# Moving the output gate's weight splits and the sums of the keys' squares to later steps of a mixer's recurrence

## The chip, the cores and the metric

The kernel runs on one core of a Trainium2 chip. Its engines are TensorE (matmul; PE in the profile, its weight loads PEld), VectorE (DVE), ScalarE (ACT), GpSimd (POOL) and SyncE (SP), whose queue issues the DMAs. The metric is the device time of one execution in microseconds; less is better.

## The reference, cut to what matters

Two layers over 128 context tokens and 256 latent tokens (384 in all, 1024 wide), each of them a feed-forward half-step, a token mixer and a second feed-forward half-step. The change is in the mixer, which computes three things from one input projection and joins them in one output projection:

```
z = h @ w_in ; zq, zi, zff, zfb, zg, zglu, cq, ck, cv = split(z)
o_a  = rms_norm(recurrence_fw + recurrence_bw) * silu(zg)        # gated linear recurrence
o_b  = silu(layer_norm(depthwise_conv(glu_a * sigmoid(glu_b))))  # convolution over 31 positions
o_c  = attention(rope(rms_norm(cq)), rope(rms_norm(ck)), cv)     # 8 query heads, 2 key heads
y    = concat(o_a, o_b, o_c) @ w_out
```

`zg` is the output gate. The RMS norm of the keys needs, for each token and key head, the sum of the 64 squares.

## The kernel before, in words

All activations lie on the chip. Each fp32 weight is split into a rounded part and a rest, and a product is three matmuls (high by high, high by low, low by high). Such a split (`prep(n, eng)`, or `wo_prep(k)` for the output weights) is a cast of 128x1024 on ScalarE (L893 in `hi`, L600) and a subtraction on VectorE (L899 in `lo`, L601). Its source is a raw buffer of 1 MB, which SyncE's queue fills. There are four raw buffers under one name (`raw`), which weights, the convolution's blocks (`cw`) and its shifted data (`U[ct]`, written to DRAM at L997 and read back at L1002) share; a buffer is handed on when its last reader is done. Split weights lie in four buffers (`wgu`).

The order of work on TensorE, VectorE, ScalarE and GpSimd is the order in which the program is written; SyncE's queue is ordered by the framework. An instruction waits in its engine's queue for what it needs, and all behind it wait too.

The 384 tokens are three blocks of 128. The recurrence is computed for two pairs of heads (`dec[0]`, `dec[1]`). For each pair, `level(8)`, `level(16)`, `level(32)` and `level(64)` rescale queries and keys with copies on ScalarE (L1123, L1124) and products on VectorE (L1127 to L1130). Then a loop of seven steps `i` does, for pair `i // 3` and token block `i % 3`:

- `scores(i)`: small matmuls (L1200) into one of two PSUM pairs, and four masked copies on VectorE (`copy_predicated`, L1209) into two tiles of scores, `a1` (three of the copies) and `a2` (one);
- `outputs(i - 1)`: matmuls (L1234) of those tiles, first `a2`, then `a1`, with the values, and of the states; after the third block a copy of the result `oS` on ScalarE (L1238);
- besides, by the number of the step: the last levels of the second pair (steps 0 and 1), the convolutions `conv(0)` and `conv(1)` (L1009, steps 2 and 4), the scaling and rotation of the keys (`norm_rope`, L953 to L961, steps 2 to 4), the turn of the second pair's keys `kN` (L1141, L1147, step 3), the states (L1155, step 4), `gh`'s load (step 3), the output weights' loads `wo_load(4)` (step 2, L1410) and `wo_load(6)`, `(0)`, `(2)` (step 5), the splits `wo_prep(4)` and `wo_prep(5)` (step 4), and in step 5 the product for the gate, `zg` (L664), which reads the split weights W[14] and W[15]. Two more `zg` follow in the attention.

Before the change `prep(14)` and `prep(15)`, the splits of the gate's weights, stand in step 0. The sums of squares (`head_ssq`: a square on ScalarE at L936, a reduction on VectorE at L937, and on GpSimd a scaling at L940 and a power at L943), one for each token block, stand ahead of the loop; `norm_rope` reads their results. In what follows a "mixer" is the first or the second layer's (about 330 to 500 us and 1080 to 1250 us of the span).

Of the kernel before, what the change touches and what calls it, by code (L numbers as in the profile page):

```python
# [18 lines left out]
P = 128  # L19
DM = 1024  # L20
KT = 8
NT = 3
# [22 lines left out]
class Net:  # L45
# [815 lines left out]
    def mixer(self, l, eps, nxt):  # L861
# [12 lines left out]
        mp = scope(es, "mix")  # L874
# [29 lines left out]
        def prep(n, eng, pool=None):  # L904
            lo(n, hi(n, pool))
# [11 lines left out]
        kn = self.t(mp, [P, NT, P], "kn")  # L917
# [14 lines left out]
        def head_ssq(x, nh, t1):  # L932

            f = 64 if nh == 8 else 1
            ss = self.t(mp, [P, 16], "ss", bufs=8)
            nc.scalar.activation(t1, x, AF.Square)  # L936
            nc.vector.reduce_sum(  # L937
                ss[:, 0:nh], t1.rearrange("p (h d) -> p h d", d=64), axis=AX.X
            )
            nc.gpsimd.tensor_scalar(  # L940
                ss[:, 0:nh], ss[:, 0:nh], f / 64, f * 1e-6, ALU.mult, ALU.add
            )
            nc.gpsimd.tensor_tensor(  # L943
                ss[:, 8 : 8 + nh], ss[:, 0:nh], self.eps[:, 2:3].to_broadcast([P, nh]), ALU.pow
            )
            return ss
# [191 lines left out]
        def state_turn(p):  # L1138
            pt = self.wbank()
            for i, (d, tok) in enumerate(((0, 0), (0, 1), (1, 0), (1, 2))):  # L1140
                nc.tensor.transpose(  # L1141
                    pt[:, i * P : (i + 1) * P],
                    dec[p].Kc[d][:, tok * P : (tok + 1) * P],
                    self.ident,
                )
            kN = self.t(hp, [P, 4, P], "kN")
            nc.scalar.copy(kN.rearrange("p a b -> p (a b)"), pt)  # L1147
            return kN

        def states(p, kN):  # L1150
            pt = self.wbank()
            for i, tok in enumerate((0, 1, 0, 2)):
                for hh in range(2):
                    rs = slice(64 * hh, 64 * hh + 64)
                    nc.tensor.matmul(  # L1155
                        pt[rs, i * 64 : i * 64 + 64],
                        kN[:, i, rs],
                        vN[:, tok, 128 * p + 64 * hh : 128 * p + 64 * hh + 64],
                        start=True,
                        stop=True,  # L1160
                    )
            S1 = self.t(hp, [P, 4, 64], "S1", bufs=2)
            for i, d in ((0, 0), (2, 1)):
                nc.scalar.copy(S1[:, i, :], pt[:, i * 64 : i * 64 + 64])
                nc.sync.dma_start(
                    self.o["new_state_hgrn"][0, l, d, 2 * p : 2 * p + 2].rearrange(
                        "h d e -> (h d) e"
                    ),
                    S1[:, i, :],
                )  # L1170
            for i, d in ((1, 0), (3, 1)):
                nc.vector.scalar_tensor_tensor(
                    S1[:, i, :], S0[:, d, p, :], dec[p].et[d][:, d + 1 : d + 2],
                    pt[:, i * 64 : i * 64 + 64], ALU.mult, ALU.add,
                )
            return S1
# [3 lines left out]
        def scores(i):  # L1180

            p, tok = divmod(i, NT)
            Qd, Kd, lev = dec[p].D, dec[p].K, dec[p].lev
            tsl = slice(tok * P, (tok + 1) * P)
            a1, a2 = A1[i % 2], A2[i % 2]
            prs = [(Qd[0], Kd[0], a1), (Qd[1], Kd[1], a2)] + [(q_, k_, a1) for q_, k_ in lev]
            if i < 2:
                sbs[i] = self.pair(1 + i)  # L1190
            sb = sbs[i % 2]
            for kd_, m, x in ((0, 32, 0), (1, 32, 0), (2, 32, 0), (3, 32, 0), (4, 32, 32), (5, 64, 64)):
                n = min(kd_, 3)
                if i < 2 and n < 3:
                    m = P
                for hh in range(2):
                    rs = slice(64 * hh, 64 * hh + 64)
                    for c in range(0, P, m):
                        r = c ^ x
                        nc.tensor.matmul(  # L1200
                            sb[c : c + m, hh, n * P + r : n * P + r + m],
                            prs[kd_][1][rs, tok * P + c : tok * P + c + m],
                            prs[kd_][0][rs, tok * P + r : tok * P + r + m],
                            start=True,
                            stop=True,
                            tile_position=(64 * hh, c),
                        )
            for n in range(4):
                nc.vector.copy_predicated(  # L1209
                    prs[n][2],  # L1210
                    self.smask[:, n, :].unsqueeze(1).to_broadcast([P, 2, P]),
                    sb[:, :, n * P : (n + 1) * P],
                )
# [141 lines left out]
        k_ss = []  # L1355
# [35 lines left out]
        glu(1)  # L1391
        S1s = [states(0, kN)]
        dec[1].level(16)
        for tok in range(NT):
            k_ss.append(head_ssq(kn[:, tok, :], 2, self.t(mp, [P, P], "t1k", bufs=2)))
        nc.sync.dma_start(self.o["new_cache_v"][0, l].rearrange("s h d -> s (h d)"), kv[:, 0, :])

        wop, wraw = {}, {}
# [2 lines left out]
        def wo_load(kb):  # L1401
            raw = wraw[kb] = self.t(self.rawp, [P, 2, DM], "raw")
            if kb < 4:
                nc.sync.dma_start(
                    raw, wo[l, kb * P : (kb + 2) * P, :].rearrange("(k p) n -> p k n", p=P)
                )
            else:
                for g in range(2):
                    r0 = 512 + g * 256 + (kb - 4) * 64
                    nc.sync.dma_start(  # L1410
                        raw[64 * g : 64 * g + 64],
                        wo[l, r0 : r0 + 128, :].rearrange("(j p) n -> p j n", p=64),
                    )

        def wo_prep(k, pool, tag, size=2 * DM, lo=nc.vector):
            w = self.t(pool, [P, size], tag, F32R)[:, 0 : 2 * DM]
            w = w.rearrange("p (a n) -> p a n", a=2)
            wop[k] = self.split_to(w, wraw[k // 2 * 2][:, k % 2, :], lo)
# [3 lines left out]
        def keys_turn():  # L1422
            pt = self.wbank()
            for i, src in enumerate((kn[:, 0, :], ck[:, 0, :], kn[:, 1, :], kn[:, 2, :])):
                nc.tensor.transpose(pt[:, i * P : (i + 1) * P], src, self.ident)
            nc.scalar.copy(kT.rearrange("p a b -> p (a b)"), pt)
# [84 lines left out]
        def zg(n):  # L1511

            tok = (1, 0, 2)[n]
            ps = self.wbank()[:, 0:256]
            self.entry_mm((ps,), [[W[14], W[15]]], tok, (0,), range(KT))
            nc.scalar.copy(zs[:, tok, :], ps)
# [3 lines left out]
        def att(n):  # L1520
            units.append(Att(n))
            units[n].scores()

        for i in range(2 * NT + 1):
            if i < 2 * NT:
                scores(i)
            if i == NT + 1:
                S1s.append(states(1, kN))
            if i == NT:
                kN = state_turn(1)  # L1530
            if i == 2 * NT:
                keys_turn()
            if i == 0:
                prep(14, nc.vector)
                prep(15, nc.vector)
            if i == 2:
                wo_load(4)
            if i in CONV_AT:
                conv(CONV_AT[i])
            if i == 5:  # L1540
                wo_load(6)
                wo_load(0)
                wo_load(2)
            if i == 4:
                wo_prep(4, self.wgu, "wgu")
                wo_prep(5, self.wgu, "wgu")
            if i > 0:
                outputs(i - 1)
            if i in HFILL:
                zg(HFILL.index(i))  # L1550
            if i == NT + 1:
                o_turn(0)
            if i == 2 * NT:
                att(0)
                units[0].exp()
            if i == NT:
                es1.close()
                ap_ = scope(es, "at")
                gh = self.t(ap_, [P, 1, 256], "gh")
                nc.sync.dma_start(  # L1560
                    gh[:, 0, :], a["hgrn_norm_g"][l : l + 1, :].to_broadcast([P, 256])
                )
            if i < 2:
                dec[1].level(32 << i)
            elif i < 2 + NT:
                tok = i - 2
                norm_rope(
                    kn[:, tok, :], k_ss[tok], tok, 2, 1, self.t(mp, [P, P], "t1k", bufs=2)
                )
# [233 lines left out]
```

## Time and profile before

| | |
|---|---|
| median of 3 runs | 1535.4 us (1534.51, 1535.40, 1538.37) |
| the profiled execution's own time | 1536.49 us |
| its span | 1534.7 us |
| its mean granted TensorE clock | 0.993 |
| TensorE busy | 1508.5 us, 98% of the span |
| VectorE, ScalarE, GpSimd busy | 69%, 42%, 4% |

The profile is one execution. Times in its rows are counted from the start of the span, in us. An instruction's row may show in brackets how long its engine stood idle before it and what ended that wait; "issue" there means that nothing in the profile shows what it waited for. A granted clock of 1 is full speed.

### The profile page before, as it was taken

Reading aid. Unit: us, or ns where it says so; the run is one execution under the profiler, and the core shown is the slowest. Engines: PE = TensorE matmul, PEld = TensorE weight load, DVE = VectorE, ACT = ScalarE, POOL = GpSimd, SP = SyncE. Lnnn points to the kernel's source line nnn. Section 1 sums busy time; section 2 is a strip of 40 time slices with the busy share of each in tenths; the row PEclk is TensorE's granted clock in tenths of the full one; section 3 lists DMA queues with packets and bytes.
Section 4 is the critical chain, followed back from the end, with each engine's and each line's share of the span. In section 5 each row is a group of like instructions: output and inputs, shape, how many; then the busy total and the mean of one; then the engine's idle time right before and its main releaser. Section 6 shows DMA issues by size and latency. Waiting matters only on the chain.

```text
span 1534.7 us, 23659 instructions
## 1 busy us (share of the span) xinstructions
PE 1508.5 (98%) x9605; PEld 1345.4 (88%) x9605; DVE 1058.5 (69%) x1525; ACT 649.3 (42%) x1112; POOL 59.3 (4%) x96
## 2 busy tenths in 40 slices
PE   8999999999999999999999999999999999999997
PEld 7989999989677899999989999998986789999996
DVE  4788778679677777777676676675795786554334
ACT  3434333366475533333353333333763764332331
POOL 0000000030101000000000000000210100000001
PEclk9999999999999999999999999999999999999999
DMA  9886766423524456666535465633336146342411
GB/s 379 287 293 223 244 234 228 171 66 136 115 93 165 165 216 238 224 227 209 206 110 220 165 247 181 240 145 122 118 94 169 48 167 249 126 179 110 165 55 41
DMA packets 65732, 271.22 MB, mean 177 GB/s; under 512 B 9224, under 2 KB 15832, under 8 KB 51032
## 3 DMA queue, kind: packets, MB, share of 16 engines
q1 hardware_dynamic: 65624, 269.72, 50.0%
q8 instruction: 75, 1.23, 0.3%
q14 instruction: 33, 0.27, 0.1%
HBM read 266.67 MB, written 3.03 MB: 176 GB/s over the span
## 4 chain that ended last, share of the span: by engine, by line
PE 93%; ACT 2%; DVE 2%; DMA 2%; issue 1%; SPq 0%; POOL 0%; DVEq 0%; POOLq 0%; ACTq 0%
PE w L610 46%; PE d L623 26%; PE d L683 7%; PE d L610 4%; PE w L1009 2%; PE w L664 1%; DMA raw<-w_mod_first 1%; PE w L208 1%; PE d L1200 1%; PE w L427 1%; PE d L1234 1%; ACT Pr L1468 1%; DVE G L196 1%; PE d L1450 1%; PE d L1498 1%
## 5 line engine op out<-in xcount | busy, mean ns | idle before, releaser
L610 PE MATMUL w<-xh,wgu 128*128 128x384 f32 x2720 | 711.9, 337 | 1.0 <-DVE hf L781 1.0
L610 PEld LDWEIGHTS w<-xh,wgu 128*128 128x128 f32 x2720 | 494.3, 188 | 10.5 <-issue 4.9
L610 PE MATMUL w<-xl,wgu 128*128 128x384 f32 x1360 | 455.9, 335 | 0.0
L623 PE MATMUL d<-wo,hh 128*128 128x512 f32 x1056 | 284.3, 391 | 0.0
L196 DVE SCALAR_TENSOR_TENSOR G<-t,cc,G 128x1024 f32<-128x1024 f32 x224 | 272.9, 1280 | 0.0
L610 PEld LDWEIGHTS w<-xl,wgu 128*128 128x128 f32 x1360 | 256.5, 189 | 2.2
L623 PEld LDWEIGHTS d<-wo,hh 128*128 128x128 f32 x1056 | 196.9, 188 | 36.5
L601 DVE TENSOR_TENSOR wgu<-raw,wgu 128x1024 fp32r<-128x1024 f32 x166 | 196.0, 1222 | 35.5 <-ACT wgu L600 35.1
L783 ACT CAST hh<-hf 128x384 fp32r<-128x384 f32 x82 | 42.2, 515 | 345.6 <-DVE hf L781 345.6
L781 DVE TENSOR_TENSOR hf<-w,sg 128x384 f32<-128x384 f32 x79 | 44.0, 557 | 185.2 <-PE w L610 185.2
L600 ACT CAST wgu<-raw 128x1024 fp32r<-128x1024 f32 x166 | 166.2, 1050 | 1.6 <-DMA raw<-ffn_w_in 1.6
L623 PE MATMUL d<-wo,hl 128*128 128x512 f32 x528 | 163.2, 390 | 0.0
L779 ACT ACTIVATE sg<-w 128x384 f32<-128x384 f32 x79 | 38.8, 491 | 265.1 <-PE w L610 265.1
L623 PEld LDWEIGHTS d<-wo,hl 128*128 128x128 f32 x528 | 99.1, 188 | 21.2
L601 DVE TENSOR_TENSOR wo<-raw,wo 128x1024 fp32r<-128x1024 f32 x90 | 109.7, 1219 | 7.6 <-ACT wo L600 7.6
L683 PE MATMUL d<-wgu,xh 128*128 128x512 f32 x336 | 104.6, 392 | 0.0
L600 ACT CAST wo<-raw 128x1024 fp32r<-128x1024 f32 x90 | 94.5, 1050 | 7.8 <-DMA raw<-ffn_w_out 7.3
L784 DVE TENSOR_TENSOR hl<-hf,hh 128x384 fp32r<-128x384 f32 x82 | 45.8, 559 | 47.7 <-ACT hh L783 47.7
L683 PEld LDWEIGHTS d<-wgu,xh 128*128 128x128 f32 x336 | 62.3, 188 | 12.5
L683 PE MATMUL d<-wgu,xl 128*128 128x512 f32 x168 | 65.6, 390 | 0.0
L436 ACT ACTIVATE t<-w,colB,colA 128x128 f32<-128x128 f32 x120 | 43.6, 470 | 46.3 <-PE w L427 38.7
L486 POOL TENSOR_TENSOR st<-st,eps 128x1 f32<-128x1 f32 x18 | 8.0, 446 | 1202.1 <-ACT X L482 1202.1
(279 smaller groups left out, 1515.2 us busy)
## 6 DMA issues: line engine op xcount, KB each, us to landing
raw<-ffn_w_in SPq DMA_DIRECT2D x78, 1024.0 KB
t<-w_mod SPq DMA_DIRECT2D x128, 512.0 KB
raw<-ffn_w_out SPq DMA_DIRECT2D x44, 1024.0 KB
raw<-w_in SPq DMA_DIRECT2D x12, 1024.0 KB
raw<-entry SPq DMA_DIRECT2D x10, 1024.0 KB
raw<-w_mod_first SPq DMA_DIRECT2D x8, 1024.0 KB
G<-gates SPq DMA_DIRECT2D x12, 512.0 KB
raw<-w_in_vk SPq DMA_DIRECT2D x4, 1024.0 KB
```

The costliest lines, as they stand in the source:

```text
L196: nc.vector.scalar_tensor_tensor(ac, raw, cc, ac, ALU.mult, ALU.add)
L436: self.nc.scalar.activation(m[:, k, :], pts[k // 4][:, k % 4 * P : (k % 4 + 1) * P], AF.Identity, scale=A[:, k, c : c + 1], bias=B[:, k, c ...
L600: nc.scalar.copy(w[:, 0], src)
L601: lo_engine.tensor_tensor(w[:, 1], src, w[:, 0].bitcast(F32), ALU.subtract)
L610: nc.tensor.matmul(ps, w[:, wi, k, :], x[:, k, :], start=(k == 0 and i == 0), stop=(k == KT - 1 and i == 2),)
L623: nc.tensor.matmul(acc[:, n, :], h, w[:, wi, n * 512 : n * 512 + 512], start=(first and i == 0), stop=(last and i == 2),)
L683: self.nc.tensor.matmul(ps, x[:, k, tok * P : (tok + 1) * P], w[k // 2][:, wi, k % 2, :], start=(k == 0 and i == 0), stop=(k == KT - 1 and ...
L779: nc.scalar.activation(sg, pg, AF.Silu)
L781: nc.vector.tensor_mul(hf, pu, sg)
L783: nc.scalar.copy(hh, hf)
L784: nc.vector.tensor_sub(hl, hf, hh.bitcast(F32))
L1009: nc.tensor.matmul(pc_[32 * j : 32 * j + 32, :], cw[:, ct, j, m, :], U[ct][:, j, 4 * m : 4 * m + OW], start=(m == 0), stop=(m == 7), tile_ ...
```

## The change

The two splits of the output gate's weights move from step 0 to step 3 of the loop. The sums of the keys' squares move from ahead of the loop to step 1, behind `dec[1].level(64)`. No operation is added or left out.

```diff
@@ -1391,8 +1391,6 @@
         glu(1)
         S1s = [states(0, kN)]
         dec[1].level(16)
-        for tok in range(NT):
-            k_ss.append(head_ssq(kn[:, tok, :], 2, self.t(mp, [P, P], "t1k", bufs=2)))
         nc.sync.dma_start(self.o["new_cache_v"][0, l].rearrange("s h d -> s (h d)"), kv[:, 0, :])
 
         wop, wraw = {}, {}
@@ -1530,7 +1528,7 @@
                 kN = state_turn(1)
             if i == 2 * NT:
                 keys_turn()
-            if i == 0:
+            if i == 3:
                 prep(14, nc.vector)
                 prep(15, nc.vector)
             if i == 2:
@@ -1562,6 +1560,8 @@
                 )
             if i < 2:
                 dec[1].level(32 << i)
+                for tok in range(NT if i else 0):
+                    k_ss.append(head_ssq(kn[:, tok, :], 2, self.t(mp, [P, P], "t1k", bufs=2)))
             elif i < 2 + NT:
                 tok = i - 2
                 norm_rope(
```

## Rows read from the trace of the kernel before

**Rows 1.** The page: busy time by engine, DMA queues (packets, MB), chain by engine.
```profile
PE 1508.5 (98%) x9605; PEld 1345.4 (88%) x9605; DVE 1058.5 (69%) x1525; ACT 649.3 (42%) x1112; POOL 59.3 (4%) x96
...
q8 instruction: 75, 1.23, 0.3%
...
PE 93%; ACT 2%; DVE 2%; DMA 2%; issue 1%; SPq 0%; POOL 0%; DVEq 0%; POOLq 0%; ACTq 0%
```
**Rows 2.** Chain that ended last, first mixer: start, us, engine, tile, line.
```profile
397.25 1.10 DVE A L1209 x3
...
400.40 1.33 issue
```
**Rows 3.** Order of time, first mixer, VectorE and GpSimd: start, us, engine, line, operation.
```profile
396.38 0.47 DVE L937 TENSOR_REDUCE ss<-t1k 128x2 f32<-128x128 f32 x2
...
397.24 1.58 DVE L1209 COPY_PREDICATED A<-smask,d 128x256 f32<-128x256 uint8 x4
...
398.71 2.35 DVE L899 TENSOR_TENSOR wgu<-raw,wgu 128x1024 fp32r<-128x1024 f32 x2
...
400.07 1.56 POOL L943 TENSOR_TENSOR ss<-ss,eps 128x2 f32<-128x2 f32 x1
```
**Rows 4.** Order of time, first mixer, TensorE.
```profile
396.58 0.64 PE L1200 MATMUL d<-db 64*32 64x32 f32 x40
...
398.05 0.44 PE L1234 MATMUL d<-A,vN 128*64 128x128 f32 x4 [0.84 <-DVE A L1209]
...
398.87 0.44 PE L1234 MATMUL d<-A,vN 128*64 128x128 f32 x4 [0.38 <-DVE A L1209]
...
402.13 6.82 PE L1009 MATMUL w<-raw,raw 128*32 128x399 f32 x64
```
**Rows 5.** Order of time, second mixer, TensorE and VectorE.
```profile
1148.56 0.44 PE L1234 MATMUL d<-A,vN 128*64 128x128 f32 x4 [0.38 <-DVE A L1209]
...
1150.74 5.57 PE L1009 MATMUL w<-raw,raw 128*32 128x399 f32 x64 [0.65 <-PE d L1200]
...
1158.64 1.59 DVE L1209 COPY_PREDICATED A<-smask,d 128x256 f32<-128x256 uint8 x4 [1.95 <-PE d L1200]
...
1163.10 5.57 PE L1009 MATMUL w<-raw,raw 128*32 128x399 f32 x64 [1.06 <-issue]
```
**Rows 6.** Windows: stretch, its length, busy us by engine, granted clock, DMA share, GB/s.
```profile
399.31:401.73 2.42, 1.09 (x87) 0.91 (x87) 2.42 (x6) 0.95 (x5) 2.23 (x2) 0.91 0.37 95
...
401.80:404.80 3.00, 3.00 (x22) 1.04 (x26) 2.96 (x12) 0.80 (x3) 0.00 (x0) 0.51 1.07 209
...
1150.74:1156.31 5.57, 5.57 (x66) 2.44 (x68) 5.50 (x22) 1.23 (x4) 0.57 (x1) 1.00 0.80 179
```
**Rows 7.** DMA, GB/s in 40 slices, 396:400 and 1147:1151; instruction queue, 399:400.
```profile
GB/s 154 188 188 154 137 240 257 188 223 154 171 188 291 257 188 223 274 223 223 138 259 207 190 311 302 390 309 234 232 147 69 202 21 0 0 0 0 0 0 0
...
GB/s 188 206 154 171 188 154 86 137 188 308 154 188 154 171 205 291 206 206 291 275 206 206 276 224 241 281 405 322 278 245 260 202 135 145 117 64 44 23 8 8
...
q8 instruction: 1, 0.02, 6.6%
```
**Rows 8.** Order of time, SyncE's queue, output weights' loads, both mixers.
```profile
401.65 1.31 SPq L1410 DMA_DIRECT2D raw<-w_out  x2
...
1163.22 1.26 SPq L1410 DMA_DIRECT2D raw<-w_out  x2
```
**Rows 9.** Second mixer, order of time; last, GB/s of 1163:1173 in slices.
```profile
1159.20 0.59 ACT L1147 COPY kN<-w 128x512 f32<-128x512 f32 x1 [2.24 <-PE w L1141]
...
1169.22 1.98 ACT L600 CAST wgu<-raw 128x1024 fp32r<-128x1024 f32 x2
...
1174.07 1.59 DVE L1209 COPY_PREDICATED A<-smask,d 128x256 f32<-128x256 uint8 x4
...
1175.88 0.66 PE L1234 MATMUL d<-A,vN 128*64 128x128 f32 x8
...
GB/s 29 103 49 82 66 0 131 131 115 0 180 344 442 262 213 164 213 213 262 213 262 197 180 246 197 98 82 148 66 16 213 410 426 393 442 442 410 410 393 442
```

## The prediction

> **What bounds the kernel now.** I read the page first. TensorE is busy for 98% of the span and the chain that ended last lies on it for 93% [rows 1], so an edit of ACT, VectorE or the queue counts only where TensorE stands still for it. The moved work sits in the mixer, once per layer. So I read the chain of waits through the first mixer [rows 2], to see where TensorE gave the chain away. Between the end of the second step of the recurrence's scores and the first convolution it does so twice: VectorE's masked copies (L1209) hold it from 397.25 on, and 1.33 us after 400.40 stand under "issue", a wait for nothing that the profile shows.
>
> Then VectorE's order of time [rows 3]. Behind level 16, without a gap, come the three reductions of the squares from 396.38 on, then step 0's four masked copies from 397.24, then two weight splits from 398.71. TensorE [rows 4] is past scores(1) at 397.22 (396.58 + 0.64), gets the first half of outputs(0) at 398.05, when two of the four copies are done, and the second at 398.87, when all are: idle 0.84 and 0.38. The second mixer repeats this to the hundredth [rows 5], but there the convolution waits 0.65 besides.
>
> **The change part by part.** *Squares out of the way.* Three reductions and a gap between them stand from 396.38 to 397.24 [rows 3]. Without them the copies start 0.86 us earlier: they need scores(0), which TensorE left before scores(1), and VectorE is free of level 16 by then. Outputs(0) would start its first half as soon as TensorE leaves scores(1) (397.22; the two copies are ready at 397.19), its second at 398.01, and end at 398.45 instead of 399.31. So 0.86 us of TensorE's 1.22 us go, in each mixer; 0.36 us stay, because all four copies must be done and only 0.86 us came free ahead of them.
>
> *Where the squares go.* Behind level 64 in step 1: three squares on ACT, three reductions on VectorE (0.86 us before, with their gap), six small operations on GpSimd, no DMA. Their first reader is the scaling of the keys in step 2. VectorE stands idle after that for 1.95 us in the second mixer, until step 3's scores [rows 5], and longer in the first. GpSimd's slowest power took 1.56 us [rows 3]; against it stand the 1.6 us of step 2's masked copies, which VectorE does between reductions and scaling, and then that idle time. Cost on the path: 0. Were that cover gone, VectorE would wait at most for one scaling and one power on GpSimd, some 3 us at twice the slowest, of which the copies hide half: 1.5 us.
>
> *The two splits.* Two casts on ACT and two subtractions on VectorE (2.35 us [rows 3]; two such casts take 1.98 [rows 9]) leave step 0 and come back in step 3, each with one predecessor: the cast behind the copy of kN, the subtractions behind step 3's masked copies. What leaves step 0 pulls the levels 32 and 64 and the copies of steps 1 and 2 forward on VectorE, by 2.35 us for the splits and, until the squares come, 0.86 more; TensorE waits for none of these, since the convolution (5.57 us, [rows 5]) stands between scores(2) and outputs(1). In step 3 the splits push the copies of oS, and on VectorE the key scaling of token 1 and the copies of step 4, back by about 2.4 us. The copies of step 4 follow its scores, and their reader, outputs(4), stands behind the second convolution, which starts at 1163.10 and takes 5.57 us [rows 5]: more than 2.4 for the splits and 1.6 for the copies. The gate's product, which needs the split weights, comes after outputs(4). Cost: 0; without the convolution it would be about 2.4 us.
>
> *The load behind the splits.* The split weights' raw buffer comes free when the second subtraction is done, and the first output weights' load is issued just behind it: subtractions end at 401.06, issue at 401.65 [rows 3, 8]. With the splits in step 3 that buffer is freed at about 1163.2 in the second mixer (kN's copy from 1159.20, 0.59 us, [rows 9]; a cast, 1; two subtractions, 2.35). But the next such load (L1410 again, 1163.22) was issued while the second convolution still ran, whose blocks and data hold two buffers; the only buffer free for it was the data of the first convolution. So a load takes the first buffer that comes free, and I take it that this load now takes that one, at 1156.3 in the second mixer (1150.74 + 5.57). Its consumer is the cast at 1169.22 [rows 9]. The comparable load issued at 1163.22 had moved its 1 MB by about 1170.5 (its traffic, summed over the slices of 0.25 us from 1165.5), 7.3 us, an estimate from [rows 9]. So the data are there at 1163.6, with 5.6 us to spare; in the first mixer the second convolution does not wait its 1.06 us [rows 5], which leaves about 4.5. Price 0; the other answer is rival 4. SP may issue the load behind others than before; it has these 4.5 us for that.
>
> *What becomes of 0.86 us at the convolution.* In the first mixer the data for it had stopped flowing by 399.3 [rows 7], so only the 1.33 us "issue" stand in between. One instruction packet of q8 moved in 399 to 400, shortly before [rows 7]; q8 carries 1.23 MB in 75 packets [rows 1], and TensorE's 19210 instructions are the only stream of that size. I take the stall for a late block of TensorE's own instructions, asked for at a fixed place of the stream, so that it moves forward with the stream. The bounds are 0 (it ends at a fixed time) and 0.86; I take 0.86, as the packet went just when outputs(0) let TensorE go on.
>
> The Trainium skill ("Runtime: NRT & Kernel Launch", Instruction fetch mechanics) says that an engine fetches its next 16 KiB block while it runs the current one, and that this is mostly hidden. The packet's size agrees with the rows; the 1.33 us do not look hidden. By the page the stall would have another cause, and the gain could be 0 instead of 0.86.
>
> In the second mixer the data came later: they flow until about 1150.6, just before the convolution starts at 1150.74 [rows 5, 7]. TensorE would be there at 1149.3 and wait 1.5 us instead of 0.65. Gain 0; the bound is 1.5, all of that wait, if the data came sooner, as in the first mixer, where they are there before the convolution's turn.
>
> *The clock.* In the first mixer the granted clock was 0.51 from 401.8 to 404.8, the lower of its two levels (1.2 GHz), and the convolution took 6.82 us against 5.57 in the second, where the clock was 1.00 [rows 4 to 6]. Before it fell TensorE was busy for 1.09 of 2.42 us. With 0.86 us of idleness less it may not fall: gain 0 to 1.25. I take 0, as the longest single idle time stays.
>
> **Sum.** First mixer -0.86, second 0, the rest 0. The profiled execution took 1536.5 us, 1.8 more than its span; it would take 1535.6. It lies 1.1 above the median of 1535.4, so the forecast is 1535.4 - 0.9 = **1534.5 us**, no difference that can be measured: about 0.3% (4.6 us) is what a measurement of this kernel tells from no change, and the three runs before differ by 3.9.
>
> **The rivals.**
>
> 1. *The clock stays up in the first mixer*: another -1.25, **1533.3 us**. For it: less idleness. Against it: 1.33 us in one piece remain. 0.22.
>
> 2. *The gain is swallowed in both mixers*, because the 1.33 us end with something that does not move: **1535.4 us**, the change does nothing. 0.17.
>
> 3. *The clock falls in the second mixer.* There the wait before the convolution grows from 0.65 to 1.5 us, and in the first a fall followed 1.33 us: +1.25 against -0.86, **1535.8 us**. Against it: the wait of 1.06 us at 1163.10 cost no clock, and the busy work ahead is only moved together. 0.08. "TensorE: Matmul & The Clock Gate" in the Trainium skill (HAM oscillation) says that waiting gaps let the clock fall to 1.2 GHz and that the work behind them then starts slow; the first mixer agrees (0.51), the second does not (1.00).
>
> 4. *The other side: the output weights' load keeps its old buffer* and follows the splits. In the second mixer: freed at 1163.2, the data 7.3 us later, 1170.5, 1.3 us after the cast could start at 1169.22. In the first mixer the 1.06 us of waiting before the second convolution are not there, so 2.4 late. VectorE's splits and the copies of step 5 are late by as much, and TensorE's outputs(5) has 0.22 us of room (copies end at 1175.66, read at 1175.88 [rows 9]). TensorE waits 1.1 + 2.2 = 3.3 us: 1535.4 - 0.9 + 3.3 = **1537.8 us**, and 1540.3 if the clock falls each time by 1.25. It is slower by more than 0.3% from an average lateness of 3 us ((4.6 + 0.9)/2 + 0.2). Against it: the buffer that the second load evidently took. 0.08.
>
> The likeliest has the remaining 0.45. The range: down to both gains at their bounds (-2.1 and -1.5), 1531.8; up to rival 4 with the clock falling once and the scatter of the runs, 1538.8. Chances: faster by over 0.3% 0.03, within 0.92, slower 0.05, the last from rival 4 and one part scatter.
>
> **What would show it.** Right: VectorE's masked copies directly behind level 16; outputs(0) idle about 0.4 in both; in the first mixer the convolution 0.9 us earlier, in the second at the same time behind a longer wait; the output weights' load issued at the end of the first convolution; no wait of ACT for it. Wrong: a cast of output weights that waits for DMA, a convolution in the first mixer that starts no earlier, a granted clock under 1 in the second, or scaled keys (L953) that wait for GpSimd with TensorE behind them.

## The result, and the profile after

The changed kernel took 1546.9 us in the median (1538.5 to 1552.6, 6 runs), the kernel before 1535.0 beside it (1531.5 to 1538.4, 6 runs): a ratio of 1.0077, 95% interval 1.0056 to 1.0098. It is slower by 0.8%. I had forecast 1534.5 us and no difference, with 0.05 for slower; the time lies outside my range of 1531.8 to 1538.8.

The profiled execution is the fastest of the six, 1538.5 us with a span of 1536.7. So it shows only a part of the loss, but it shows where. The page is nearly that of before [rows 1]: TensorE does the same work in the same time, and its share of the chain that ended last fell from 93% to 91%. Two lines of the page (busy time by engine; chain by engine):

```profile
PE 1508.4 (98%) x9605; PEld 1344.2 (87%) x9605; DVE 1058.7 (69%) x1525; ACT 648.9 (42%) x1112; POOL 55.7 (4%) x96
...
PE 91%; DVE 3%; ACT 2%; DMA 2%; issue 1%; SPq 0%; POOL 0%; DVEq 0%; POOLq 0%; ACTq 0%
```

TensorE's order of time, first mixer and then second (start, us, line, tiles; in brackets the idle time and what ended it):

```profile
395.55 0.44 PE L1234 MATMUL d<-A,vN 128*64 128x128 f32 x4 [0.37 <-DVE A L1209]
...
398.62 0.47 PE L1200 MATMUL d<-db 64*64 64x64 f32 x2 [1.55 <-issue]
399.03 6.89 PE L1009 MATMUL w<-raw,raw 128*32 128x399 f32 x64
...
415.53 0.78 PE L1200 MATMUL d<-db 64*32 64x32 f32 x24 [4.76 <-issue]
...
417.29 6.29 PE L1009 MATMUL w<-raw,raw 128*32 128x399 f32 x64
...
1150.86 0.44 PE L1234 MATMUL d<-A,vN 128*64 128x128 f32 x4 [0.37 <-DVE A L1209]
...
1152.82 5.57 PE L1009 MATMUL w<-raw,raw 128*32 128x399 f32 x64 [0.43 <-DMA raw<-ud]
...
1165.08 5.57 PE L1009 MATMUL w<-raw,raw 128*32 128x399 f32 x64 [0.95 <-DMA raw<-ud]
```

The reader is to see three things. Outputs(0) lost 0.84 us of its idle time in both mixers, as the change was to do [rows 4, 5]. A new stand of 4.76 us under "issue" lies in the middle of scores(4) of the first mixer; before, TensorE had no stand of 0.3 us or more in steps 3 and 4 of that mixer (in the second it had one of 1.06 us ahead of the second convolution [rows 5]). And the second convolution behind it took 6.29 us instead of 5.57. The same place before:

```profile
413.34 0.93 PE L1200 MATMUL d<-db 64*32 64x32 f32 x38
...
414.81 5.57 PE L1009 MATMUL w<-raw,raw 128*32 128x399 f32 x64
```

The windows of the same stretch (length, busy us by engine, granted clock, DMA share, GB/s) show the surroundings of that stand:

```profile
405.90:410.80 4.90, 4.87 (x192) 3.78 (x188) 1.85 (x5) 2.44 (x4) 0.00 (x0) 1.00 1.03 217
410.80:415.50 4.70, 0.00 (x0) 0.00 (x0) 3.44 (x7) 1.00 (x2) 0.00 (x0) 0.99 0.55 107
415.50:417.30 1.80, 1.77 (x42) 1.47 (x42) 0.92 (x3) 0.00 (x0) 0.00 (x0) 0.50 0.03 9
417.30:423.60 6.30, 6.30 (x68) 2.11 (x68) 0.99 (x4) 0.33 (x2) 0.00 (x0) 0.88 0.56 122
```

Ahead of the stand the DMA engines are full (1.03, 217 GB/s). Behind it the granted clock is 0.50, the lower level of 1.2 GHz. SyncE's queue, by order of time, says whose bytes these are:

```profile
402.27 0.33 SPq L1570 DMA_DIRECT2D new_cache_k<-kn  x1
402.70 1.81 SPq L1002 DMA_DIRECT2D raw<-ud  x4
405.99 1.31 SPq L1408 DMA_DIRECT2D raw<-w_out  x2
```

The first output weights' load (L1408, 1 MB) is issued at 405.99, right when the first convolution ends (399.03 + 6.89 = 405.92), and not at 401.65 as before [rows 8]. The second convolution's data (L1002) come at 402.70, behind the store of the new keys, for which the queue had waited. Before, nearly all of this flowed under the first convolution; now most of it flows under scores(3) and scores(4). The window of the first convolution before:

```profile
401.73:408.95 7.22, 7.22 (x68) 2.46 (x70) 5.16 (x19) 0.87 (x3) 0.00 (x0) 0.79 1.06 217
```

The loss in the profile adds up. From the first matmul of outputs(0) to the end of the second convolution the first mixer took 28.85 us (22.33 before) and the second 20.59 (20.93 before). The changed kernel starts outputs(0) 0.84 us earlier in its stream, so against the same point it lost 28.85 - 0.84 - 22.33 = 5.7 us in the first mixer and gained 1.2 in the second. Outputs(0) itself began at 394.74, 2.5 us ahead of 398.05 - 0.84, from scatter in code that the change doesn't touch: 5.7 - 1.2 - 2.5 = 2.0 us, and the two profiled executions differ by 2.0 (1538.5 to 1536.5). What the other five runs lost besides had to be seen in a second look at the same kernel (below).

### The profile page after: what moved, and what is told of

It reads as the page before. It is cut to its first block, busy times and chain, and to the rows that moved or that the text cites. A ratio compares the mean times of both kernels' runs of the same rounds, so it can differ in the third digit from the quotient of the medians.

```text
span 1536.7 us, 23657 instructions
## 1 busy us (share of the span) xinstructions
PE 1508.4 (98%) x9605; PEld 1344.2 (87%) x9605; DVE 1058.7 (69%) x1525; ACT 648.9 (42%) x1112; POOL 55.7 (4%) x96
## 3 DMA queue, kind: packets, MB, share of 16 engines
q8 instruction: 75, 1.23, 0.3%
## 4 chain that ended last, share of the span: by engine, by line
PE 91%; DVE 3%; ACT 2%; DMA 2%; issue 1%; SPq 0%; POOL 0%; DVEq 0%; POOLq 0%; ACTq 0%
PE w L610 45%; PE d L623 26%; PE d L683 7%; PE d L610 4%; PE w L1009 1%; PE w L664 1%; PE w L208 1%; DMA raw<-w_mod_first 1%; PE w L427 1%; DVE G L196 1%; PE d L1448 1%; PE d L1496 1%; PE d L1234 1%; PE w L1485 1%; DMA raw<-ffn_w_out 0%
## 5 line engine op out<-in xcount | busy, mean ns | idle before, releaser
L600 ACT CAST wgu<-raw 128x1024 fp32r<-128x1024 f32 x166 | 166.0, 1049 | 1.4 <-DMA raw<-ffn_w_in 1.4
L600 ACT CAST wo<-raw 128x1024 fp32r<-128x1024 f32 x90 | 94.4, 1049 | 8.0 <-DMA raw<-ffn_w_out 7.5
L610 PE MATMUL d<-xh,wgu 128*128 128x384 f32 x192 | 51.4, 340 | 0.3 <-ACT wgu L600 0.3
```

What stands on the lines that cost most here:

```text
L600: nc.scalar.copy(w[:, 0], src)
L610: nc.tensor.matmul(ps, w[:, wi, k, :], x[:, k, :], start=(k == 0 and i == 0), stop=(k == KT - 1 and i == 2),)
```

## The experiments

Four explanations stood at first. **Q**: the store of the new keys, which now stands ahead of the second convolution's data in SyncE's queue, sends those data late. **B**: the output weights' load comes late and its bytes flow under the instruction-rich steps, where they hold up TensorE's own instructions. **C**: the squares in step 1. **D**: the splits on ScalarE and VectorE in step 3 hold TensorE directly. Each run was timed in rounds beside the kernel before (1533.9, 1533.7, 1533.7 and 1533.3 us in the four sets).

The stands in the last column are those of the one profiled execution of each run, in us. In the profile of the kernel before they are under 0.3 and 1.06.

| run | median us | ratio to before, interval | largest stand in steps 3 and 4, first and second mixer |
|---|---|---|---|
| squares only | 1533.4 | 0.9997, 0.9986 to 1.0008 | under 0.3, 0.3 |
| splits only | 1547.1 | 1.0092, 1.0077 to 1.0107 | 4.46, 4.65 |
| changed, store behind the loads | 1541.1 | 1.0055, 1.0041 to 1.0069 | 4.42, 3.39 |
| changed, once more | 1541.0 | 1.0053, 1.0035 to 1.0071 | 5.71, 3.14 |
| changed, without the load | 1532.2 | 0.9987, 0.9976 to 0.9997 | 0.56, under 0.3 |
| before, with a copy of 1 MB in step 2 | 1537.1 | 1.0022, 1.0010 to 1.0033 | 1.44, 1.80 |
| before, with a copy of 2 MB in step 2 | 1543.0 | 1.0053, 1.0040 to 1.0065 | 3.71, 2.84 |
| before, with a copy of 1 MB late | 1533.7 | 0.9996, 0.9983 to 1.0010 | 0.40, under 0.3 |
| changed, load and its splits late | 1535.4 | 1.0006, 0.9995 to 1.0016 | under 0.3, under 0.3 |
| squares only, load and its splits late | 1535.9 | 1.0011, 0.9998 to 1.0024 | 0.42, under 0.3 |

**Each part of the change by itself.** The squares only:

```diff
         dec[1].level(16)
-        for tok in range(NT):
-            k_ss.append(head_ssq(kn[:, tok, :], 2, self.t(mp, [P, P], "t1k", bufs=2)))
...
             if i < 2:
                 dec[1].level(32 << i)
+                for tok in range(NT if i else 0):
+                    k_ss.append(head_ssq(kn[:, tok, :], 2, self.t(mp, [P, P], "t1k", bufs=2)))
```

> Only the squares move; the splits stay in step 0, and SyncE's order is that of the kernel before. Theory Q (the splits' move lets the store of the new keys pass ahead of the second convolution's data in SyncE's queue; the data and the output weights' load then flow over steps 3 and 4, where TensorE's instruction blocks stand behind them): no slowdown, -0.9 to 0 us against before, the outputs(0) gain of 0.86 in the first mixer intact. Rival B (the output weights' load is late because its buffer is another): the same, -0.9 to 0. Rival C (the squares behind level 64 delay the keys): +2 to +12 us.

1533.4 us, no difference: C falls. The trace also shows where the 0.84 us went. Order of time on TensorE, first and second mixer:

```profile
394.72 0.44 PE L1234 MATMUL d<-A,vN 128*64 128x128 f32 x4 [0.37 <-DVE A L1209]
...
398.01 0.33 PE L1200 MATMUL d<-db 64*64 64x64 f32 x2 [1.77 <-issue]
...
1147.11 7.18 PE L1009 MATMUL w<-raw,raw 128*32 128x399 f32 x64 [1.49 <-DMA raw<-ud]
```

The stand ahead of the first convolution grew from 1.33 to 1.77 us [rows 2]. In the second mixer the convolution waited 1.49 us instead of 0.65 [rows 5], by the profile for its data, and then ran 7.18 us, with a granted clock of 0.50 for its first 3.3 us. The work comes earlier, and what it waits for doesn't.

The splits only:

```diff
-            if i == 0:
+            if i == 3:
                 prep(14, nc.vector)
                 prep(15, nc.vector)
```

> Only the splits move; the squares stay ahead of the loop. The store of the new keys stands ahead of the second convolution's data in SyncE's queue as in the changed kernel. Theory Q: slower by about as much as the changed kernel, +6 to +15 us, with a wait of several us under issue in steps 3 or 4 of a mixer. Rival B: the same, +6 to +15. Rival C (the squares): within 2 us of before.

1547.1 us: more than the whole loss, 13.3 us against the 7.1 that the changed kernel lost in the same set ("once more" in the table). The squares' move, which does nothing alone, gives back some 6 us here. Why was not tested; in this run's profile, its slowest execution of five, both mixers' first convolutions, too, ran partly at the lower clock (a granted 0.65 over 8.47 us and 0.76 over 7.26 us). TensorE's order of time, both mixers:

```profile
419.63 0.78 PE L1200 MATMUL d<-db 64*32 64x32 f32 x24 [4.46 <-issue]
...
1176.30 2.22 PE L1009 MATMUL w<-raw,raw 128*32 128x399 f32 x12 [4.65 <-issue]
```

**The order in SyncE's queue.** The changed kernel with the store of the new keys queued behind the last load, as before:

```diff
-                nc.sync.dma_start(
+                wraw["last"] = nc.sync.dma_start(
...
-        nc.sync.dma_start(self.o["new_cache_k"][0, l].rearrange("s h d -> s (h d)"), kn[:, 0, :])
+        with tc.issue_after(wraw["last"].ins):
+            nc.sync.dma_start(
+                self.o["new_cache_k"][0, l].rearrange("s h d -> s (h d)"), kn[:, 0, :]
+            )
```

> The changed kernel with the store of the new keys queued behind the last output weights' load of step 5, as before; the output weights' first load still takes the first convolution's buffer and flows during steps 3 and 4. Theory Q: most of the loss is gone, -1 to +4 us against before, the second convolution's data read at once when their write has landed. Rival B (the late output weights' load does it): still +6 to +15. Rival D (splits on ACT and VectorE in step 3 do it directly): still +6 to +15.

1541.1 us, the same as the unaltered changed kernel on that chip (1541.0, next run). In its queue the second convolution's data are asked for at 398.15 again, and the output weights at 405.59:

```profile
398.15 1.75 SPq L1002 DMA_DIRECT2D raw<-ud  x4
405.59 1.30 SPq L1408 DMA_DIRECT2D raw<-w_out  x2
```

The stand in scores(4) stays (4.42 us). Q falls: the order of the store does not make the loss. What is left of it here is the late load, or the splits themselves (D).

The changed kernel once more, for a profile of an ordinary run:

> The changed kernel once more, as a control on the same chip and for a second profile. All theories: +5 to +15 us against before, with a granted clock lower in the longer runs; theory Q: the extra time lies in steps 3 and 4 of the mixers, as waits under issue that end about 1.5 us after an instruction packet, and in stretches at the lower clock behind them.

```profile
416.24 0.78 PE L1200 MATMUL d<-db 64*32 64x32 f32 x24 [5.71 <-issue]
...
1168.46 2.11 PE L1009 MATMUL w<-raw,raw 128*32 128x399 f32 x16 [3.14 <-DMA raw<-ud]
```

Both mixers have a stand here, 5.71 and 3.14 us, and each is followed by a fallen clock. So the second mixer, which got through in the first profile, mostly does not. The wait in front of its second convolution is put down to the data, which did land last there (the instruction packet before it had ended 3.3 us earlier); in the run with the splits alone the same place stands under "issue", 1.5 us behind a packet. In that mixer data and instructions come late together, and which of them was last changes from run to run.

**Taking the load away, and moving it.** From here on theory T is B, sharpened: whatever flows while TensorE runs steps 3 and 4 holds up its instructions. The changed kernel without the first output weights' load (GpSimd fills the buffer):

```diff
             raw = wraw[kb] = self.t(self.rawp, [P, 2, DM], "raw")
...
                 for g in range(2):
+                    if kb == 4:
+                        nc.gpsimd.memset(raw[64 * g : 64 * g + 64], 0.0)
+                        continue
```

> The changed kernel without the first output weights' load (L1408 in step 2): its raw buffer is filled with zeros by GpSimd instead, so 1 MB less flows in each mixer; output weights 4 and 5 are left out of the computation. Theory T (the load's traffic over the third and fourth step of the scores holds up TensorE's instruction packets): the stands of 4 to 6 us under "issue" in scores(4) shrink to under 2 us in both mixers, and the time comes down to 1531 to 1537 us. Rival D (the splits themselves, on ACT and VectorE in step 3, hold TensorE): the time stays at 1538 to 1547 us. If a stand of 2 us or more stays, the second convolution's data alone do a part of it.

1532.2 us: with the splits still in step 3 the loss is gone, and the stand in scores(4) is 0.56 us. (Its profile is that of its slowest execution of twelve, 1540.9 us; the first convolutions took 8.35 and 8.32 us there, with a clock that fell.)

```profile
416.15 0.57 PE L1200 MATMUL d<-db 64*32 64x32 f32 x24 [0.56 <-issue]
```

D falls here. The same is seen with all the work in place, when the load is issued behind the state's stores of step 4 (and its two splits are moved behind the first exponentials; the store of the new keys stands behind the loads as above):

```diff
-            if i == 2:
-                wo_load(4)
...
             if i == 5:
+                with tc.issue_after(sto[1].ins):
+                    wo_load(4)
                 wo_load(6)
...
-            if i == 4:
-                wo_prep(4, self.wgu, "wgu")
-                wo_prep(5, self.wgu, "wgu")
...
                 units[0].exp()
+                wo_prep(4, self.wgu, "wgu")
+                wo_prep(5, self.wgu, "wgu")
```

> The changed kernel, with the first output weights' load queued behind the state's stores of step 4 (from about 417 us in the first mixer, when the second convolution's turn is there) and its two splits moved from step 4 to behind the first exponentials of the attention; the new keys' store is queued behind the last load of output weights. Theory T: no stand of over 2 us in scores(3) or scores(4); 1530 to 1538 us, where the upper end is for the splits (some 2 us on ACT and 2.4 on VectorE in each mixer) if the attention has no room for them. Rival D (the splits of step 3 themselves): 1538 to 1547 us.

1535.4 us. Windows of TensorE over steps 3 and 4 and up into the second convolution: busy for 9.80 of 10 us at a clock of 1.00, with the DMA engines at 0.10:

```profile
405.00:415.00 10.00, 9.80 (x280) 6.11 (x276) 5.49 (x12) 3.78 (x7) 0.00 (x0) 1.00 0.10 23
```

Against the same point as above this kernel is ahead of the kernel before by 1.8 us in the first mixer and 2.7 in the second at the end of the second convolution (21.39 and 19.07 us from outputs(0)). It gives that back. In its order of time there is a stand in step 6, where the output weights now flow, and a wait behind the two casts:

```profile
427.20 0.32 PE L1236 MATMUL d<-da,S 64*64 64x128 f32 x1 [1.86 <-issue]
...
433.89 0.51 PE L664 MATMUL w<-wgu,xh 128*128 128x256 f32 x2 [0.54 <-ACT zs L1516]
```

The same with the gate's splits back in step 0, that is, the squares moved, and the load and its splits late. One more thing differs from the run before it: the store of the new keys isn't held behind the loads, and goes out at 404.00, with the second convolution's data asked for ahead of it (396.38).

> The run before this one with the output gate's splits back in step 0: squares moved, load and splits of the first output weights late. Theory T: as with the splits in step 3, 1530 to 1538 us, within 2 us of it, since the load flows at the same time in both. Rival D: 4 to 10 us faster than with the splits in step 3.

1535.9 us. With the load at the same time in both, the place of the gate's splits makes no difference that was measured (0.6 us, intervals that overlap). That is the second ground on which D falls.

**Bytes that nobody waits for.** The kernel before, which has neither edit, with a copy from DRAM to DRAM behind the first output weights' load (256 rows of weights are 1 MB, 512 rows 2 MB):

```diff
+                with tc.issue_after(wraw["ld"].ins):
+                    nc.sync.dma_start(
+                        self.spare[l], wo[l, 0:256, :].rearrange("(p a) n -> p (a n)", p=P)
+                    )
```

> The kernel before, with one more transfer in each mixer: a copy of 1 MB of output weights to a place in DRAM that nobody reads, queued on SyncE's queue behind the first output weights' load in step 2. No instruction of a compute engine changes and none waits for the copy. Theory T: it flows over the steps 3 and 4, TensorE stands 2 to 5 us longer under "issue" there, and the time is 1537 to 1548 us. Rival W (only loads that somebody waits for cost time): 1533 to 1536 us, with no new stand.

> The kernel before with a copy of 2 MB instead of 1 MB behind the first output weights' load in step 2. Theory T: the traffic reaches over the whole of steps 3 and 4, TensorE's stands there grow with it, to 3 to 6 us in each mixer, and the time is 1540 to 1550 us, as with the late load of the changed kernel. Rival M: twice the price of the 1 MB copy, 1540 to 1541 us, spread, without a long stand.

1537.1 us with 1 MB, at the low edge of what I expected, and 1543.0 with 2 MB: +3.4 and +9.3. The stands are 1.44 and 1.80 us with 1 MB, smaller than I had expected (the second is 0.74 more than the 1.06 us of before), and 3.71 and 2.84 with 2 MB. No instruction of a compute engine differs and none reads the copy. TensorE's order of time with 2 MB, both mixers, and then the window over steps 3 and 4 (6.93 of 10 us busy, DMA share 0.91, 290 GB/s):

```profile
415.64 0.57 PE L1201 MATMUL d<-db 64*32 64x32 f32 x24 [3.71 <-issue]
...
1167.50 2.16 PE L1010 MATMUL w<-raw,raw 128*32 128x399 f32 x12 [2.84 <-issue]
...
405.00:415.00 10.00, 6.93 (x216) 4.31 (x208) 3.56 (x12) 1.66 (x3) 0.00 (x0) 1.00 0.91 290
```

The stands lie at the same instructions as in the changed kernel: ahead of the last 24 matmuls of scores(4) in the first mixer, ahead of the second convolution in the second. So theory W, that only awaited loads cost time, falls. The control for a price by the byte (theory M) is the 1 MB copy behind the store of the new keys:

> The kernel before with the same copy of 1 MB that nobody reads, queued on SyncE's queue behind the store of the new keys instead (some 421 us in the first mixer), so that it flows under the attention, where TensorE waits for ScalarE and VectorE anyway. Theory T (it matters when the bytes flow, not that they flow): 1533 to 1536 us, no new stand in the steps of the scores. Rival M (a megabyte more costs its share of the memory wherever it flows): 3 us slower than before, as with the copy in step 2, 1536 to 1538 us.

1533.7 us, no difference: M falls. The copy was issued at 417.25 and did not only flow under the attention, as I had written, but under steps 5 and 6 first, at full DMA engines (3.06 MB in 416 to 424, 382 GB/s), and TensorE went on:

```profile
416.79 1.09 PE d L1201 x64
417.89 1.03 PE d L1235 x16
418.91 3.08 PE w L665 x24
```

**A version that beats both?** Two more placed the late load's splits in step 5, at its end and ahead of outputs(4). The second one's edit, against the run with the load late:

```diff
+            if i == 5:
+                wo_prep(4, self.wgu, "wgu")
+                wo_prep(5, self.wgu, "wgu")
             if i > 0:
                 outputs(i - 1)
```

> The changed kernel with the first output weights' load behind the state's stores of step 4, as in the earlier run of that kind, but with its two splits at the end of step 5, where ScalarE still has idle time, instead of behind the first exponentials. Theory T: no stand in scores(3) and scores(4); the wait of 0.55 us for the gate's copy in step 6 goes; 1531 to 1535 us. If the casts wait for their data there (the load lands about 6 us after it is issued), ScalarE holds up step 6 and the time is 1535 to 1539 us.

> As the run with the late load and its splits at the end of step 5, but with the splits ahead of outputs(4) in step 5, so that their casts stand in front of the copy of the gate's product in ScalarE's order, where ScalarE was idle for 4.66 us in the second mixer. Theory T: no stand in scores(3) and scores(4), the wait of 1.23 us for the keys' copy goes, the stand of 1.7 us in step 6 of the first mixer stays (the output weights' loads flow under it): 1533 to 1536 us, no measurable difference from the kernel before. If that last stand goes as well: 1530 to 1533 us, faster than both kernels. If the casts wait for the load: 1536 to 1540 us.

1536.4 us (1.0011, 0.9998 to 1.0024) and 1534.7 us (1.0003, 0.9988 to 1.0018). At the end of step 5 the casts delayed the copy of the turned keys (1.23 us of waiting in the second mixer); ahead of outputs(4) that wait was gone. In both the stand in step 6 of the first mixer stayed (1.70 and 1.45 us). In the first of the two the casts had not waited for their data, so the mechanism that I had named for 1535 to 1539 us was not the one. Neither beats the kernel before.

## Why the prediction was wrong

**What held.** The masked copies stand directly behind level 16, and outputs(0) idles 0.37 us instead of 1.22 in both mixers. The squares cost nothing. The two splits cost nothing on ScalarE and VectorE. The output weights' load took the first convolution's buffer and went out at its end; rival 4, the old buffer, did not come. No cast of output weights waited for it: in the profile after, ScalarE's casts (L600, 424.15) follow the convolution's activation directly.

**What failed: "Price 0" for the load behind the splits.** I asked only whether the 1 MB would be there for the cast that reads it, found 4.5 to 5.6 us to spare, and closed the step. The reader that counted was another one. (That the store of the new keys would pass ahead in the queue I had not seen either; by the run with the old order it cost nothing that could be measured.) TensorE's instructions come over the same DMA engines (q8 is one of the page's DMA queues [rows 1]), and in steps 3 and 4 TensorE uses them up fast. Queue lines for 399 to 412.5, before and after the change, and then for 412.5 to 414.5 after it:

```profile
q1 hardware_dynamic: 935, 1.94, 68.7%
q8 instruction: 3, 0.05, 1.6%
...
q1 hardware_dynamic: 997, 1.99, 68.1%
q8 instruction: 1, 0.02, 0.5%
...
q1 hardware_dynamic: 151, 0.13, 35.6%
q8 instruction: 1, 0.02, 4.2%
```

and then with the load late, for 399 to 412.5:

```profile
q1 hardware_dynamic: 712, 1.00, 33.0%
q8 instruction: 2, 0.03, 1.1%
```

So after the change the next packet came in 412.5 to 414.5 (at 412.73), after 2 MB of other bytes, and TensorE, which had stopped at 410.77, went on at 415.53, 1.45 us after that packet's end. The same holds in all fourteen traces: each of the 32 stands of 0.3 us or more under "issue" in 380 to 445 and 1135 to 1195 us ends 1.2 to 1.6 us after the end of a packet of q8. Waits put down to a DMA in these stretches have no such fixed distance (0.1 to 8.5 us).

The place fits a block's end too. Between the two stands of the first mixer (398.62 and 415.53) lie 2 + 64 + 16 + 88 + 4 + 16 + 64 = 254 pairs of a weight load and a matmul, 508 instructions, and 19210 instructions in 75 packets are 256 each [rows 1]: two blocks, within the few matmul records that a trace can lack. The second block begins 128 pairs behind 398.62, in scores(3) at 407.42:

```profile
407.42 0.21 PE L1200 MATMUL d<-db 64*32 64x32 f32 x1
```

If the third block is asked for when the second begins, TensorE had 3.3 us until it needed it, an estimate from these counts. Counted in the same way, the block that ends in scores(4) of the first mixer, and the packet that moves next, in us:

| run | block begins | packet moves | later by | stand at the block's end |
|---|---|---|---|---|
| before | 410.45 | 411.30 | 0.9 | under 0.3 |
| changed, without the load | 412.38 | 413.43 | 1.1 | 0.56 |
| before, with a copy of 1 MB late | 405.43 | 406.50 | 1.1 | 0.40 |
| before, with a copy of 1 MB in step 2 | 406.83 | 408.81 | 2.0 | 1.44 |
| before, with a copy of 2 MB in step 2 | 408.72 | 413.12 | 4.4 | 3.71 |
| splits only | 411.83 | 416.66 | 4.8 | 4.46 |
| changed, store behind the loads | 407.04 | 412.03 | 5.0 | 4.42 |
| changed | 407.42 | 412.73 | 5.3 | 4.76 |
| changed, once more | 407.20 | 413.45 | 6.3 | 5.71 |

From the second row on, each stand is the packet's lateness less 0.4 to 0.7 us. Under the convolution a block lasts far longer, since its 64 pairs take 5.57 us against about 1.1 for the 88 of a step of scores. That is why the same bytes were hidden there: before, the block of the first convolution began at 401.73 and its packet moved at 407.44, 5.7 us later, with the DMA engines as full (1.06); but the block lasted until 410.45, and nothing stood.

I had both halves in hand. In the first mixer I took the 1.33 us for a late block of instructions, and in [rows 9] I summed the load's traffic over 7.3 us. I used the first only to ask whether the stall moves with the stream, and not what the traffic that I was moving would do to the next blocks. The upper end of my range doesn't follow from its terms either: rival 4's 1537.8 and 1.25 for the clock are 1539.05 before any scatter, not 1538.8; the measured time lies above both. I wrote that the Trainium skill ("Runtime: NRT & Kernel Launch", Instruction fetch mechanics) calls the fetch of the next 16 KiB mostly hidden. The traces agree with the size (1.23 MB in 75 packets) and with a fetch ahead (the packet of 407.44, above). With the DMA engines full over scores(3) and scores(4) it was not hidden, by 4.4 to 5.7 us in the first mixer.

**The clock** was the second part of the loss. I had taken no change in its term. Each stand of 2.8 us or more in steps 3 and 4 is followed by a granted clock of 0.50. After the change: 0.78 us for 24 matmuls of scores(4) that take 0.57 at full clock, 1.12 instead of 0.69 for the states, 6.29 instead of 5.57 for the convolution, about 1.4 us for one stand. In the profile after, 4.8 + 1.4 less the 0.6 us gained at the first convolution (below) are 5.6 of the 5.7 us lost there. For the ordinary run (once more) this gives, from outputs(0) to the end of the second convolution and against the same point, 29.59 - 0.84 - 22.33 = 6.4 and 23.98 - 0.84 - 20.93 = 2.2 us, 8.6 in all. Its time of 1543.6 was 7.1 above the profile of before; the other 1.5 us lie outside these stretches.

**The gain at the first convolution** was mis-sized: 0.86 us forecast in the first mixer. In the changed kernel the convolution ends 0.6 us earlier against the same point (11.17 - 0.84 = 10.33 from outputs(0), 10.90 before), with the squares alone 0.0 (11.72 - 0.84 = 10.88), since the stand ahead of it grew and more of it ran at the lower clock (7.26 us against 6.82). In the second mixer I had forecast 0, with the convolution at the same time behind a longer wait. With the squares alone it came so (3.84 - 0.84 = 3.00 us from outputs(0), 3.00 before, behind 1.49 us), but the clock fell there, which was my rival 3. In the changed kernel the convolution began 1.1 us earlier instead (2.77 - 0.84 = 1.93), behind 0.43 us. Of my rivals, numbers 2 (the gain is swallowed) and 3 are nearest to what the squares do by themselves.

**Still open.** The profile doesn't show when a packet is asked for, only when it moves, so that it waits behind the data is worked out from its lateness and from the copies, not seen. In step 6 of the kernel with the load late the block begins at 419.15 and its packet moves at 424.43, 5.3 us later, and TensorE stands 1.9 us; in the kernel with the late copy the block begins at 416.81 and its packet moves at 417.99, 1.2 us later, and nothing stands. The DMA engines are full in both stretches (1.03 and 1.10), so a full share alone doesn't make a packet late; what else does is open. So is why the splits alone cost 6 us more than the whole change, and why the changed kernel lost 0.8% in the first measurement and 0.5% in the second.

## What to carry to other kernels

A transfer has more readers than the instruction that waits for its data: while it fills the DMA engines, an engine that runs many short instructions can run out of them. So when an edit moves a buffer's release, ask in which stretch the next load into it will flow, and let it flow under long instructions. A stand under "issue" at an unchanged instruction, with full DMA engines ahead of it and one packet of the instruction queue that ends 1.2 to 1.6 us before TensorE goes on, is the mark of it here; a copy that nobody reads, put into the unchanged kernel, tests it in one run.

## What was not expected of the hardware

- 1 MB more on the DMA engines, read by nobody, cost the kernel 3.4 us when it flowed under steps 3 and 4, 2 MB there cost 9.3 us, and 1 MB some 18 us later cost nothing that could be measured.
- TensorE stood up to 5.7 us for its own instructions, in a kernel that is straight-line code, and each time went on 1.2 to 1.6 us after a packet of its instruction queue had ended.
